# The gate products of a recurrent mixer as pairs of 64-row products in the two halves of the TensorE array

## The chip, the cores and the metric

The kernel runs on one core of a Trainium2 chip. The metric is the time of one launch on the device in microseconds (us), smaller is better. The median of the runs is what counts.

## The reference, cut to what matters

The reference is a decoder trunk of two layers on 512 positions of 1024 channels: FFN, token mixer and FFN in each layer, and a norm at the end. The change lies in the token mixer of layer 0, a gated linear recurrence:

```
def block_diag_linear(x, w, b):          # 16 heads of 64 channels
    xh = x.reshape(bsz, s, h, dh)
    return (jnp.einsum('bshi,hij->bshj', xh, w) + b).reshape(bsz, s, h * dh)
...
gate_a = sigmoid(block_diag_linear(x, w_a, b_a))
gate_x = sigmoid(block_diag_linear(x, w_x, b_x))
log_a = -8 * gate_a * softplus(-lam);  a = exp(log_a)
bx = x * gate_x * sqrt(-expm1(2 * log_a))
h[t] = a[t] * h[t-1] + bx[t]
```

Here x is the right half of `hn @ w_in` after a causal convolution of width 4. The left half goes through a GELU, is multiplied by h, and the product goes through `w_out`. Each head of 64 channels has a 64x64 matrix for gate a and one for gate x.

## The kernel before, in words

All matrices lie in single precision. To multiply them with TensorE's faster type, each operand is split into a high and a low part: ScalarE copies it to `hi` with rounding, VectorE subtracts to get `lo`, and three matmuls (hi·hi, lo·hi, hi·lo) sum into one PSUM bank (`mm3`, L242 to L245). Weights come by DMA into `raw` tiles and are split into `whi` and `wlo`; activations are split into tiles named `hi` and `lo` (`split`, L116).

The program is a list of steps (`subs`), each one block of weights. The loop at the end runs them in order. A step issues, on each engine in program order: the hooks of phase "pre", the split of the weights of the step three ahead, the hooks "mid" and "rest", the step's own matmuls, and then the hooks "end" and "late". Every engine works through its own queue in that order, so the place of a hook decides what stands behind what. A weight block must be split before its step's matmuls, and a bank must have been read before the next product is written to it. Six PSUM banks (`bank`) are given out in turn to the products and the gates.

The recurrent mixer (`recurrent`, L1198) is tiled by channel blocks c = 0..7 of 128 channels, two heads each, channels on the partitions and the 512 positions along the free dimension. Its first twelve steps make the right half of `hn @ w_in`. Blocks 0 to 3 come in two halves of 256 positions, blocks 4 to 7 in one step of 24 matmuls each (tile `r`). When block c is done, `r_post` (L1220) starts a chain over the following steps:

- ScalarE writes `rc` (the last tap of the convolution with its bias), and VectorE adds the other three taps (`taps`, "late").
- One step later ("mid") `rc` is split into `hi` and `lo`.
- At the end of that step or of the next one, `gate` puts two gate products on TensorE, one for a and one for x. Each uses a 128x128 weight tile with two heads' 64x64 matrices on its diagonal and zeros beside them, and each is three matmuls of 128 rows, 128 columns and 512 positions: 6 for a block, 48 in all. The weight tiles are made by `load_gate`: zeros from GpSimd, then DMAs into the diagonal blocks, four tiles of 128x512 in all, each split once (`split_gate`).
- One step after that ("mid") ScalarE takes the two `sigmoids` (tile `g`) with the gate's bias from the table of vectors `vec`, and a tanh of gate a (tile `tl`).
- Another step later VectorE multiplies `rc` by gate x (`product`, tile `pr`).

Within "mid" of one step, the sigmoids of an earlier block stand ahead of the split of a later block's `rc`. On TensorE gates 0, 1 and 2 each stand after the product of a later block, gates 3 and 4 back to back after block 5's, gate 5 after block 6's, and gates 6 and 7 back to back after the first product of the left half: six groups.

The recurrence itself is a list by hand (`plan`, L1301): `exp_` on ScalarE, `oma2` on VectorE (squares and products, tiles `a` and `tl`), square roots on ScalarE, `scan` on VectorE, GELUs on ScalarE, products `yh` on VectorE, and splits of them. They feed the product with `w_out`, seven products of a Strassen scheme with banks named A, B and C, that comes after the eight steps of the left half.

Of the kernel before, what the change touches and what calls it, by code (L numbers as in the profile page):

```python
# [11 lines left out]
AF = mybir.ActivationFunctionType  # L12
ALU = mybir.AluOpType

P = 128
# [10 lines left out]
V_F1, V_MIX, V_F2, V_CW, V_CB, V_GA, V_GX, V_LAM, V_SB = 0, 16, 32, 48, 80, 88, 96, 104, 112  # L26
# [44 lines left out]
def trunk(ctx: ExitStack, tc: tile.TileContext, a: dict, out: bass.AP):  # L71
    nc = tc.nc
# [28 lines left out]
    def f32(t):  # L101
        return t.bitcast(F32)

    def tt(o, x, y, op):
        nc.vector.tensor_tensor(out=o, in0=x, in1=y, op=op)  # L105
# [4 lines left out]
    def stt(o, x, s, y, op0, op1):  # L110
        nc.vector.scalar_tensor_tensor(out=o, in0=x, scalar=s, in1=y, op0=op0, op1=op1)  # L111

    def act(o, x, f, **k):
        nc.scalar.activation(out=o, in_=x, func=f, **k)  # L114

    def split(src):  # L116

        w = src.shape[-1]
        hi, lo = slot(F32R, "hi")[:, :w], slot(F32R, "lo")[:, :w]
        act(hi, src, AF.Copy)  # L120
        tt(lo, src, f32(hi), ALU.subtract)
        return hi, lo
# [110 lines left out]
    def hook(n, phase, fn):  # L233


        hooks.setdefault((n, phase), []).append(fn)
# [5 lines left out]
    def mm3(ps, wh, wl, xh, xl, start, stop):  # L242
        nc.tensor.matmul(ps, wh, xh, start=start, stop=False)  # L243
        nc.tensor.matmul(ps, wh, xl, start=False, stop=False)  # L244
        nc.tensor.matmul(ps, wl, xh, start=False, stop=stop)  # L245
# [17 lines left out]
    def vcol(row):  # L263
        return vec[:, row : row + 1]
# [933 lines left out]
    def recurrent(w_in, w_out, norm):  # L1198
        gates = {}

        def load_gate(name, q):
            g = gates[name, q] = slot(name="gw")
            nc.gpsimd.memset(g, 0.0)
            gv = g.rearrange("p (c j) -> p c j", c=4)
            wv = a[f"rec_gate_{name}_w"][0, q * 8 : (q + 1) * 8].rearrange("(c two) i j -> two i c j", two=2)
            for two in range(2):
                nc.sync.dma_start(out=gv[two * 64 : (two + 1) * 64, :, two * 64 : (two + 1) * 64], in_=wv[two])

        def split_gate(name, q):
            gates[name, q] = split(gates[name, q])  # L1210

        at0 = len(subs)
        y0 = at0 + 12
        for n, (name, q) in enumerate((name, q) for q in range(2) for name in ("a", "x")):
            hook(at0 + (-9,-8,-2,-1)[n], "late", lambda name=name, q=q: load_gate(name, q))
            hook(at0 + (-3,-2,3,4)[n], "mid", lambda name=name, q=q: split_gate(name, q))

        rc, ga, gx, tl, pr, ym = {}, {}, {}, {}, {}, {}

        def r_post(c, ps):  # L1220
            n = now[0]
            g = n + (2 if c < 4 or c == 6 else 1)
            v = rc[c] = slot(name="rc")
            hl, pss = [], []
            act(v, ps, AF.Identity, scale=vcol(V_CW + 24 + c), bias=vcol(V_CB + c))

            def taps():
                for k in (0, 1, 2):
                    stt(v[:, 3 - k :], ps[:, : T - 3 + k], vcol(V_CW + 8 * k + c), v[:, 3 - k :], ALU.mult, ALU.add)

            def gate():
                for name in "ax":
                    pg = bank("gate")
                    wh, wl = gates[name, c // 4]
                    cs = slice((c % 4) * P, (c % 4 + 1) * P)
                    mm3(pg, wh[:, cs], wl[:, cs], hl[0], hl[1], True, True)
                    pss.append(pg)
                hl.clear()

            def sigmoids():  # L1240
                for dst, brow in ((ga, V_GA), (gx, V_GX)):
                    dst[c] = slot(name="g")
                    act(dst[c], pss.pop(0), AF.Sigmoid, bias=vcol(brow + c))
                tl[c] = slot(name="tl")
                act(tl[c], ga[c], AF.Tanh, scale=lru_c[:, c : c + 1])

            def product():
                pr[c] = slot(name="pr")
                tt(pr[c], rc.pop(c), gx.pop(c), ALU.mult)

            hook(n, "late", taps)
            hook(n + 1, "mid", lambda: hl.extend(split(v)))
            hook(g, "end", gate)
            hook(g + 1, "mid", sigmoids)
            hook(g + 2, "mid", product)

# [272 lines left out]
    def lru_consts():  # L1529
# [44 lines left out]
        for i in range(13, 0, -2):  # L1574
# [73 lines left out]
    def vec_rest():  # L1648

        nc.vector.memset(stage[:V_ROWS, :P], 0.0)  # L1650
        for src, r0, n in rows:
            flat = src.rearrange("h d -> (h d)") if len(src.shape) == 2 else src.rearrange("o h d -> (o h d)")
            nc.gpsimd.dma_start(out=stage[r0 : r0 + n, :P], in_=flat.rearrange("(n p) -> n p", p=P))

    def vec_rest_t():
        ps = aux("vec")
# [146 lines left out]
```

## Time and profile before

| what | value |
|---|---|
| time, median of 3 runs | 1561.8 us (1561.55 to 1561.82) |
| the profiled execution, first to last instruction | 1559.5 us |
| instructions | 21004 |
| TensorE matmuls busy | 1551.9 us, 7293 matmuls |
| VectorE busy | 1309.5 us |
| ScalarE busy | 1188.7 us |
| GpSimd busy | 245.3 us |
| granted TensorE clock, mean | 0.999 |
| the recurrent mixer's gates on TensorE | from 350.9 to 392.0 us |

The profile holds one execution; of it the span is recorded and no other time, and the runs' median lies 2.3 us above that span. In the views PE is TensorE's matmuls, PEld its weight loads, DVE VectorE, ACT ScalarE, POOL GpSimd and SP the engine that issues most DMAs. A row of a timeline gives start, duration, engine, line, operation, output and inputs, shape and count, and in brackets the idle time of the engine before it with what ended it. Durations overlap: the next instruction of an engine starts before the one before has ended, so the cost of one among many is the distance between starts. Helpers hide lines (every ScalarE activation is L114), so tiles are the better guide.

### The profile page before, as it was taken

How to read it: one execution, taken by the hardware profiler on the slowest of the kernel's cores; microseconds unless marked ns; L12 is line 12 of the kernel's file. 1: busy time of each engine (PE TensorE's matmuls, PEld its weight loads, DVE VectorE, ACT ScalarE, POOL GpSimd, SP SyncE). 2: the span in 40 equal slices, each digit the busy share in tenths (PEclk: the TensorE clock that was granted, in tenths of full speed). 3: DMA queues.
4: the chain of work that ended last, by engine and by line, in shares of the span. 5: the costliest groups of instructions: out<-in, count | busy, mean ns of one | idle time of the engine just before them, and what ended most of it. 6: DMA issues, size and time to landing. Idle time of an engine off the chain costs nothing.

```text
span 1559.5 us, 21004 instructions
## 1 busy us (share of the span) xinstructions
PE 1551.9 (100%) x7293; PEld 1318.4 (85%) x7293; DVE 1309.5 (84%) x1776; ACT 1188.7 (76%) x1777; POOL 245.3 (16%) x220
## 2 busy tenths in 40 slices
PE   9999999999999999999999999999999999999998
PEld 7888888898888998888889988888888889888886
DVE  6977789888999777789897877798879997777998
ACT  7877787668778868796877787867787877778856
POOL 2111112300020111112211111122211111111220
PEclk9999999999999999999999999999999999999999
DMA  9888899953395988899977888989878859898994
GB/s 315 189 189 196 186 217 229 228 137 109 103 230 137 191 199 198 189 232 224 244 179 183 188 203 185 227 227 238 224 191 219 203 138 216 197 212 177 241 235 138
DMA packets 268763, 310.53 MB, mean 199 GB/s; under 512 B 111232, under 2 KB 149232, under 8 KB 268656
## 3 DMA queue, kind: packets, MB, share of 16 engines
q1 hardware_dynamic: 214368, 210.02, 46.4%
q0 software_dynamic: 52496, 97.33, 37.0%
q10 hardware_dynamic: 1792, 1.84, 0.4%
q8 instruction: 57, 0.93, 0.2%
q14 instruction: 50, 0.41, 0.1%
HBM read 282.39 MB, written 2.10 MB: 182 GB/s over the span
## 4 chain that ended last, share of the span: by engine, by line
PE 98%; DVE 1%; DMA 0%; ACT 0%; issue 0%; SPq 0%; DVEq 0%
PE A L479 15%; PE A L478 15%; PE A L480 15%; PE C L480 8%; PE C L479 8%; PE C L478 8%; PE B L479 4%; PE B L480 4%; PE B L478 4%; PE r L243 2%; PE r L244 2%; PE r L245 2%; PE Q L480 2%; PE Q L479 2%; PE Q L478 2%; PE p L958 1%
## 5 line engine op out<-in xcount | busy, mean ns | idle before, releaser
L105 DVE TENSOR_TENSOR wlo<-raw,whi 128x1024 fp32r<-128x1024 f32 (+2 forms) x567 | 651.9, 1153 | 208.3 <-ACT whi L114 206.7
L114 ACT ACTIVATE whi<-raw 128x1024 fp32r<-128x1024 f32 (+2 forms) x567 | 564.4, 1001 | 239.0 <-DVE raw L105 93.1
L478 PE MATMUL A<-whi,hi 128*128 128x512 f32 (+1 forms) x1104 | 421.0, 381 | 0.0
L479 PE MATMUL A<-whi,lo 128*128 128x512 f32 (+1 forms) x1104 | 419.3, 380 | 0.1
L480 PE MATMUL A<-wlo,hi 128*128 128x512 f32 (+1 forms) x1104 | 419.3, 380 | 0.0
L478 PEld LDWEIGHTS A<-whi,hi 128*128 128x128 f32 x1104 | 207.3, 188 | 35.9 <-ACT c L114 1.0
L480 PEld LDWEIGHTS A<-wlo,hi 128*128 128x128 f32 x1104 | 207.2, 188 | 35.6
L479 PEld LDWEIGHTS A<-whi,lo 128*128 128x128 f32 x1104 | 207.3, 188 | 35.4 <-DVE lo L105 0.5
L156 POOL DMA_DIRECT2D raw<-in_ffn_w_in_dram x100 | 120.7, 1207 | 710.1 <-DVE raw L105 322.8
L478 PE MATMUL C<-whi,hi 128*128 128x512 f32 (+1 forms) x608 | 231.4, 381 | 0.0
L479 PE MATMUL C<-whi,lo 128*128 128x512 f32 (+1 forms) x608 | 231.3, 380 | 0.0
L480 PE MATMUL C<-wlo,hi 128*128 128x512 f32 (+1 forms) x608 | 231.3, 380 | 0.0
L156 POOL DMA_DIRECT2D raw<-in_ffn_w_out_dram x73 | 83.8, 1194 | 319.1 <-DVE wlo L105 199.2
L105 DVE TENSOR_TENSOR raw<-raw,raw 128x1024 f32<-128x1024 f32 (+1 forms) x113 | 131.0, 1159 | 1.1
L479 PEld LDWEIGHTS C<-whi,lo 128*128 128x128 f32 x608 | 114.1, 188 | 20.1 <-DVE lo L105 0.2
L478 PEld LDWEIGHTS C<-whi,hi 128*128 128x128 f32 x608 | 114.2, 188 | 19.9
L480 PEld LDWEIGHTS C<-wlo,hi 128*128 128x128 f32 x608 | 114.1, 188 | 19.9
L105 DVE TENSOR_TENSOR lo<-a,hi 128x512 fp32r<-128x512 f32 (+1 forms) x184 | 119.7, 658 | 1.4 <-ACT hi L114 1.3
L114 ACT ACTIVATE hi<-a 128x512 fp32r<-128x512 f32 (+1 forms) x184 | 107.8, 596 | 14.5 <-DVE a L105 12.8
L114 ACT ACTIVATE c<-A 128x512 f32<-128x512 f32 (+1 forms) x150 | 81.9, 567 | 46.5 <-PE A L480 46.1
L479 PE MATMUL B<-whi,lo 128*128 128x512 f32 (+1 forms) x304 | 115.7, 381 | 0.2 <-DVE lo L111 0.2
L478 PE MATMUL B<-whi,hi 128*128 128x512 f32 (+1 forms) x304 | 115.7, 381 | 0.0
(189 smaller groups left out, 1964.5 us busy)
## 6 DMA issues: line engine op xcount, KB each, us to landing
raw<-in_ffn_w_in_dram SPq DMA_DIRECT2D x143, 512.0 KB, 5.6
raw<-in_ffn_w_out_dram SPq DMA_DIRECT2D x98, 512.0 KB, 5.7
raw<-in_ffn_w_in_dram POOLq DMA_DIRECT2D x76, 512.0 KB, 7.7
raw<-in_ffn_w_out_dram POOLq DMA_DIRECT2D x58, 512.0 KB, 7.6
raw<-in_ffn_w_in_dram SPq DMA_DIRECT2D x48, 384.0 KB, 4.2
raw<-in_sg_w_in_dram SPq DMA_DIRECT2D x20, 512.0 KB, 7.0
raw<-in_ffn_w_in_dram POOLq DMA_DIRECT2D x24, 384.0 KB, 6.3
raw<-in_rec_w_in_dram SPq DMA_DIRECT2D x16, 512.0 KB, 5.4
```

Source lines behind the costliest of these rows:

```text
L105: nc.vector.tensor_tensor(out=o, in0=x, in1=y, op=op)
L114: nc.scalar.activation(out=o, in_=x, func=f, **k)
L156: nc.gpsimd.dma_start(out=self.v, in_=src, accum_op=ALU.add)
L243: nc.tensor.matmul(ps, wh, xh, start=start, stop=False)
L244: nc.tensor.matmul(ps, wh, xl, start=False, stop=False)
L245: nc.tensor.matmul(ps, wl, xh, start=False, stop=stop)
L478: nc.tensor.matmul(ps, zh, wh, start=fresh and i == 0, stop=False, **k)
L479: nc.tensor.matmul(ps, zl, wh, start=False, stop=False, **k)
L480: nc.tensor.matmul(ps, zh, wl, start=False, stop=end, **k)
L958: nc.tensor.matmul(bank_of(half, s), z, (sub.lo if m == 2 else sub.hi)[:, q, :], start=left[2] == "2" and (h, q, m) == (0, 0, 0), stop=lef ...
```

## The change

The a and x matrices of one head are put side by side: a weight tile now has, in its rows 0 to 63, the even head's a in columns 0 to 63 and its x in columns 64 to 127, and in its rows 64 to 127 the odd head's x in columns 0 to 63 and its a in columns 64 to 127. There are no zeros left, so GpSimd's memsets go, and two weight tiles take the place of four, with two splits instead of four. A block's six gate matmuls become three pairs: the even head with rows 0 to 63 of the array into one bank, the odd head with rows 64 to 127 into another. Each has 64 rows, 128 columns and 512 positions. A bank now holds a and x of one head, so each gate is gathered by two activations of 64 partitions each: for a from the same partitions, for x from the other half. So there are four sigmoids for a block instead of two. The bias of gate x lies in `vec` with its halves exchanged, by two small DMAs at the start. The four gate DMAs of one half of the heads are issued at one place.

```
-                for name in "ax":
-                    pg = bank("gate")
-                    wh, wl = gates[name, c // 4]
-                    cs = slice((c % 4) * P, (c % 4 + 1) * P)
-                    mm3(pg, wh[:, cs], wl[:, cs], hl[0], hl[1], True, True)
-                    pss.append(pg)
+                pss.extend(bank("gate") for _ in range(2))
+                cs = slice((c % 4) * P, (c % 4 + 1) * P)
+                for m in range(3):
+                    for two in range(2):
+                        rows = slice(two * 64, (two + 1) * 64)
+                        nc.tensor.matmul(pss[two], gates[c // 4][m == 2][rows, cs], hl[0][m == 1][rows, :],
+                                         start=m == 0, stop=m == 2)
                 hl.clear()
 
             def sigmoids():
-                for dst, brow in ((ga, V_GA), (gx, V_GX)):
-                    dst[c] = slot(name="g")
-                    act(dst[c], pss.pop(0), AF.Sigmoid, bias=vcol(brow + c))
+                for dst, brow, n in ((ga, V_GA, 0), (gx, V_GX, 1)):
+                    g = dst[c] = slot(name="g")
+                    for two in range(2):
+                        o = (two ^ n) * 64
+                        act(g[two * 64 : (two + 1) * 64], pss[two][o : o + 64], AF.Sigmoid, bias=vcol(brow + c)[o : o + 64])
+                pss.clear()
...
-            g = gates[name, q] = slot(name="gw")
-            nc.gpsimd.memset(g, 0.0)
+            g = gates[q] = slot(name="gw")
...
-            for two in range(2):
-                nc.sync.dma_start(out=gv[two * 64 : (two + 1) * 64, :, two * 64 : (two + 1) * 64], in_=wv[two])
+            for n, name in enumerate("ax"):
+                wv = a[f"rec_gate_{name}_w"][0, q * 8 : (q + 1) * 8].rearrange("(c two) i j -> two i c j", two=2)
+                for two in range(2):
+                    o = (two ^ n) * 64
+                    nc.sync.dma_start(out=gv[two * 64 : (two + 1) * 64, :, o : o + 64], in_=wv[two])
...
-        for n, (name, q) in enumerate((name, q) for q in range(2) for name in ("a", "x")):
-            hook(at0 + (-9,-8,-2,-1)[n], "late", lambda name=name, q=q: load_gate(name, q))
-            hook(at0 + (-3,-2,3,4)[n], "mid", lambda name=name, q=q: split_gate(name, q))
+        for q in range(2):
+            hook(at0 + (-9, -2)[q], "late", lambda q=q: load_gate(q))
+            hook(at0 + (-3, 3)[q], "mid", lambda q=q: split_gate(q))
```

On TensorE, gate 0 (tiles `gate`, inputs `hi` and `lo` of `rc` and the split gate weights) stands before as two products of three matmuls, one bank after the other:

```order
L243 MATMUL gate_3463<-hi_3394,hi_3112 128x512
L244 MATMUL gate_3463<-lo_3395,hi_3112 128x512
L245 MATMUL gate_3463<-hi_3394,lo_3113 128x512
L243 MATMUL gate_3467<-hi_3394,hi_3134 128x512
L244 MATMUL gate_3467<-lo_3395,hi_3134 128x512
L245 MATMUL gate_3467<-hi_3394,lo_3135 128x512
```

Now it stands as three pairs, the two banks in turn, and both products read the same weight tile (`hi_3110`, `lo_3111`), one in its upper and one in its lower rows:

```order
L1239 MATMUL gate_3450<-hi_3381,hi_3110 128x512
L1239 MATMUL gate_3451<-hi_3381,hi_3110 128x512
L1239 MATMUL gate_3450<-lo_3382,hi_3110 128x512
L1239 MATMUL gate_3451<-lo_3382,hi_3110 128x512
L1239 MATMUL gate_3450<-hi_3381,lo_3111 128x512
L1239 MATMUL gate_3451<-hi_3381,lo_3111 128x512
```

The number of matmuls and their columns are as before; `lo` is first read by the third matmul of a block instead of the second.

On ScalarE, the stretch from block 5's `rc` (`rc_3644`) over the sigmoids of blocks 3 and 4 to the split of that `rc` reads before:

```order
L114 ACTIVATE rc_3644<-r_3603,vec 128x512
L114 ACTIVATE whi_3650<-raw_3094 128x1024
L114 ACTIVATE g_3656<-gate_3628,vec 128x512
L114 ACTIVATE g_3658<-gate_3632,vec 128x512
L114 ACTIVATE tl_3660<-g_3656,lru_c 128x512
L114 ACTIVATE g_3662<-gate_3636,vec 128x512
L114 ACTIVATE g_3664<-gate_3640,vec 128x512
L114 ACTIVATE tl_3666<-g_3662,lru_c 128x512
L114 ACTIVATE hi_3668<-rc_3644 128x512
```

And now, from the sigmoids on (the `rc` is `rc_3637`):

```order
L114 ACTIVATE g_3649<-gate_3621,vec 64x512
L114 ACTIVATE g_3649<-gate_3622,vec 64x512
L114 ACTIVATE g_3652<-gate_3621,vec 64x512
L114 ACTIVATE g_3652<-gate_3622,vec 64x512
L114 ACTIVATE tl_3655<-g_3649,lru_c 128x512
L114 ACTIVATE g_3657<-gate_3629,vec 64x512
L114 ACTIVATE g_3657<-gate_3630,vec 64x512
L114 ACTIVATE g_3660<-gate_3629,vec 64x512
L114 ACTIVATE g_3660<-gate_3630,vec 64x512
L114 ACTIVATE tl_3663<-g_3657,lru_c 128x512
L114 ACTIVATE hi_3665<-rc_3637 128x512
```

Four activations more stand ahead of the split of block 5 (`hi_3665`); all else keeps its order.

More of the change, by code (lines that the diff above doesn't have):

```diff
@@ L1199, in recurrent, with load_gate, split_gate @@
         gates = {}
-        def load_gate(name, q):
-            g = gates[name, q] = slot(name="gw")
-            nc.gpsimd.memset(g, 0.0)
+        def load_gate(q):
+            g = gates[q] = slot(name="gw")
             gv = g.rearrange("p (c j) -> p c j", c=4)
-            wv = a[f"rec_gate_{name}_w"][0, q * 8 : (q + 1) * 8].rearrange("(c two) i j -> two i c j", two=2)
-            for two in range(2):
-                nc.sync.dma_start(out=gv[two * 64 : (two + 1) * 64, :, two * 64 : (two + 1) * 64], in_=wv[two])
-        def split_gate(name, q):
-            gates[name, q] = split(gates[name, q])
+            for n, name in enumerate("ax"):
[3 more added lines that the diff above has]
+                    nc.sync.dma_start(out=gv[two * 64 : (two + 1) * 64, :, o : o + 64], in_=wv[two])
+        def split_gate(q):
+            gates[q] = split(gates[q])
         at0 = len(subs)
         y0 = at0 + 12
-        for n, (name, q) in enumerate((name, q) for q in range(2) for name in ("a", "x")):
-            hook(at0 + (-9,-8,-2,-1)[n], "late", lambda name=name, q=q: load_gate(name, q))
-            hook(at0 + (-3,-2,3,4)[n], "mid", lambda name=name, q=q: split_gate(name, q))
+        for q in range(2):
+            hook(at0 + (-9, -2)[q], "late", lambda q=q: load_gate(q))
+            hook(at0 + (-3, 3)[q], "mid", lambda q=q: split_gate(q))
         rc, ga, gx, tl, pr, ym = {}, {}, {}, {}, {}, {}
@@ L1251, in r_post @@
             hook(n, "late", taps)
-            hook(n + 1, "mid", lambda: hl.extend(split(v)))
+            hook(n + 1, "mid", lambda: hl.append(split(v)))
             hook(g, "end", gate)
@@ L1652, in vec_rest @@
             flat = src.rearrange("h d -> (h d)") if len(src.shape) == 2 else src.rearrange("o h d -> (o h d)")
-            nc.gpsimd.dma_start(out=stage[r0 : r0 + n, :P], in_=flat.rearrange("(n p) -> n p", p=P))
+            v = flat.rearrange("(n p) -> n p", p=P)
+            if r0 == V_GX:
+                for o in (0, 64):
+                    nc.gpsimd.dma_start(out=stage[r0 : r0 + n, o : o + 64], in_=v[:, 64 - o : 128 - o])
+            else:
+                nc.gpsimd.dma_start(out=stage[r0 : r0 + n, :P], in_=v)
     def vec_rest_t():
```

## The prediction, made before the changed kernel was run

> **What bounds the kernel now.** I read the page first: the busy times and the chain that ended last.
>
> ```profile
> span 1559.5 us, 21004 instructions
> PE 1551.9 (100%) x7293; PEld 1318.4 (85%) x7293; DVE 1309.5 (84%) x1776; ACT 1188.7 (76%) x1777; POOL 245.3 (16%) x220
> PE 98%; DVE 1%; DMA 0%; ACT 0%; issue 0%; SPq 0%; DVEq 0%
> ```
>
> TensorE carries the end nearly everywhere, so a shorter gate product looks like time won, one for one. But shares of the whole say little of one stage, so next I read the windows of 10 us over the mixer (columns: window, length, then busy time and count of PE, PEld, DVE, ACT, POOL).
>
> ```profile
> 370.00:380.00 10.00, 10.00 (x46) 8.28 (x45) 7.24 (x10) 9.97 (x16) 0.00 (x0) 1.00 0.52 126
> 380.00:390.00 10.00, 10.00 (x46) 8.29 (x45) 9.80 (x14) 8.44 (x12) 1.20 (x1) 1.00 0.22 58
> 400.00:410.00 10.00, 10.00 (x46) 8.29 (x45) 9.83 (x13) 8.86 (x11) 0.00 (x0) 1.00 0.15 50
> 430.00:440.00 10.00, 10.00 (x46) 8.29 (x45) 10.00 (x16) 6.51 (x9) 1.73 (x2) 1.00 1.02 217
> ```
>
> Here three engines are close to full: ScalarE for 9.97 of 10 us while gates 3 to 5 run, and then VectorE, up to 10.00 of 10. Before the change TensorE never waits, but those two have almost no room. The change takes work from TensorE and gives work to ScalarE, so the question is how much delay ScalarE can take.
>
> **TensorE's part.** The tile view of the gates and the timeline of PE:
>
> ```profile
> L243 PE MATMUL gate<-hi,hi x16: 389/389/396, 350.9 to 391.3; 128*128 128x512 f32 x16
> 368.88 0.39 PE L243 MATMUL gate<-hi,hi 128*128 128x512 f32 x1
> 371.60 0.39 PE L243 MATMUL r<-zh,whi 128*128 128x512 f32 x1
> ```
>
> Gates 3 and 4, twelve matmuls, take 371.60 − 368.88 = 2.72 us, 0.227 each by the distance of starts; a block's six take 1.36, all 48 take 10.9. If the two halves run side by side, a pair costs 0.227 and 24 × 0.227 = 5.4 us are saved. If they don't, 48 × 0.227 stays as it is. No row shows the array in halves, so both are ends. Going into and out of halves, a matmul may have to finish first: 0.389 − 0.227 = 0.16 us, and twelve times that (six groups) is 1.9 us more. So PE's term lies between −5.4 and +1.9. The Trainium skill, TensorEngine Tiling (Array Packing), section Theoretical Speedup, promises up to twofold for a contraction of 64 rows or less; by it alone the sum would be 1561.8 − 5.4 = 1556.4. The same page, Key Properties, says that changing the tiling mode drains TensorE; it gives no price. Which end is right matters little, as the next part shows.
>
> **ScalarE's part.** Each block gets two activations more, 16 in all, on 64 partitions by 512 columns:
>
> ```profile
> L114 ACT ACTIVATE g<-gate,vec x16: 672/688/704, 356.1 to 399.3; 128x512 f32<-128x512 f32 x16
> 356.08 1.27 ACT L114 ACTIVATE g<-gate,vec 128x512 f32<-128x512 f32 x2
> 357.24 0.72 ACT L114 ACTIVATE tl<-g,lru_c 128x512 f32<-128x512 f32 x1
> 361.73 0.65 ACT L114 ACTIVATE hi<-rc 128x512 fp32r<-128x512 f32 x1
> 362.96 1.05 ACT L114 ACTIVATE whi<-raw 128x1024 fp32r<-128x1024 f32 x1
> ```
>
> Two sigmoids hold the engine for 357.24 − 356.08 = 1.16, 0.58 each. No activation of 64 partitions is in the trace. The rows of 512 and 1024 columns (0.65 and 1.05) show that time goes with columns, and the columns stay 512; so I take the same price, 1.15 us more a block. The bounds: half of it (0.29 each, nothing added), and the whole duration without overlap (0.69 each, 1.6 us more a block).
>
> Now place by place, with what ScalarE waits for in between:
>
> ```profile
> 356.54 0.47 PE L243 MATMUL r<-zh,whi 128*128 128x512 f32 x1
> 354.07 2.31 DVE L111 SCALAR_TENSOR_TENSOR rc<-r,vec,rc 128x509 f32<-128x509 f32 x3
> 366.10 0.64 ACT L114 ACTIVATE hi<-rc 128x512 fp32r<-128x512 f32 x1 [0.32 <-DVE rc L111]
> 369.08 0.78 ACT L114 ACTIVATE rc<-r,vec 128x512 f32<-128x512 f32 x1 [2.35 <-PE r L245]
> 370.71 1.25 ACT L114 ACTIVATE g<-gate,vec 128x512 f32<-128x512 f32 x2
> 372.46 1.27 ACT L114 ACTIVATE g<-gate,vec 128x512 f32<-128x512 f32 x2
> 374.21 0.65 ACT L114 ACTIVATE hi<-rc 128x512 fp32r<-128x512 f32 x1
> 374.89 0.69 DVE L105 TENSOR_TENSOR lo<-rc,hi 128x512 fp32r<-128x512 f32 x1 [0.95 <-ACT hi L114]
> ```
>
> *Gates 0 to 3.* What PE wins at gates 0 and 1 is lost again at once: block 4's product (356.54) takes the bank whose taps end at 354.07 + 2.31 = 356.38, and these hang on VectorE, not on PE. Only 0.16 of room is there.
>
> *Gate 4.* Its `hi` (366.10) stands behind the sigmoids of blocks 0 to 2: 3 × 1.15 − 0.32 = 3.13 later, so from 369.23 to 369.87, and `lo` follows for 0.69, to 370.6. PE, with gates 2 and 3 shorter, could be there at 370.24 − 1.36 − 0.16 = 368.7 and now waits. Its second and third pair (0.45 together side by side, 0.9 otherwise) start at 370.6 and end at 371.05 to 371.5. Before it was 371.60: almost all won by then is gone.
>
> *Gate 5.* The 2.35 us that ScalarE idled before 369.08 swallow most of the 3.13 (back to back, `rc` starts 0.54 after `hi`, at 369.77, which is 0.69 late). Then come two blocks of sigmoids, 2.30: `hi` starts at 374.21 + 2.99 = 377.20, ends at 377.85, `lo` ends at 378.57.
>
> ```profile
> 377.04 0.39 PE L243 MATMUL gate<-hi,hi 128*128 128x512 f32 x1
> 378.40 0.39 PE L243 MATMUL r<-zh,whi 128*128 128x512 f32 x1
> 382.28 1.27 ACT L114 ACTIVATE g<-gate,vec 128x512 f32<-128x512 f32 x2
> 384.57 0.78 ACT L114 ACTIVATE rc<-r,vec 128x512 f32<-128x512 f32 x1
> 385.38 2.32 DVE L111 SCALAR_TENSOR_TENSOR rc<-r,vec,rc 128x509 f32<-128x509 f32 x3
> 389.35 0.68 DVE L105 TENSOR_TENSOR lo<-rc,hi 128x512 fp32r<-128x512 f32 x1
> 392.00 0.39 PE L243 MATMUL r<-zh,whi 128*128 128x512 f32 x1
> ```
>
> PE's last two pairs start at 378.6 and end at 379.05 to 379.5, against 378.40: now 0.65 to 1.1 late.
>
> *Gates 6 and 7.* From 374.21 to 384.57 no ScalarE row has idle time ahead of it, and block 5's sigmoids (382.28) add 1.15: `rc` of block 7 is 4.14 late, and with it VectorE's taps (385.38) and the `lo` of block 7 (389.35), which ends at 389.35 + 0.68 + 4.14 = 394.17. Gate 7's last two pairs end at 394.65 to 395.1 instead of 392.00: PE 2.65 to 3.1 late.
>
> *VectorE after that.* It has no idle time in the recurrence to give the delay back, and one wait is added:
>
> ```profile
> 396.96 1.27 ACT L114 ACTIVATE g<-gate,vec 128x512 f32<-128x512 f32 x2
> 398.73 1.26 ACT L114 ACTIVATE g<-gate,vec 128x512 f32<-128x512 f32 x2
> 401.91 0.72 ACT L114 ACTIVATE g<-g,lru_nc 128x512 f32<-128x512 f32 x1
> 404.38 0.67 DVE L105 TENSOR_TENSOR a<-g 128x512 f32<-128x512 f32 x1
> 418.47 0.63 ACT L114 ACTIVATE hi<-a 128x512 fp32r<-128x512 f32 x1 [5.54 <-DVE a L105]
> 439.75 0.68 DVE L105 TENSOR_TENSOR lo<-a,hi 128x512 fp32r<-128x512 f32 x1
> 441.18 0.39 PE L479 MATMUL C<-whi,lo 128*128 128x512 f32 x1
> ```
>
> The sigmoids of blocks 6 and 7 add 2.30 on ScalarE, so the exponential (401.91) is 6.44 late and ends at 409.07; VectorE's square of it (404.38), otherwise 4.14 late at 408.52, starts at 409.1: VectorE is 4.72 late. ScalarE recovers in its idle 5.54 us (418.47), VectorE doesn't. The `lo` at 439.75 ends at 440.43; the matmul that reads it started at 441.18. With 4.72 it ends at 445.15, so that matmul starts at 445.18, 4.0 late, and TensorE, 2.65 to 3.1 late by itself, waits there once more. Behind that the steps go as before, 4.0 later.
>
> **What goes at nothing.** Two splits of gate weights, four memsets and the earlier order of four small DMAs lie before 343 us, off the path: TensorE has its blocks split three steps ahead there. Their price if that cover were gone, and their gain, is at most what two splits hold, under 1.4 us.
>
> ```profile
> L114 ACT ACTIVATE hi<-gw x4: 614/637/656, 323.6 to 341.9; 128x512 fp32r<-128x512 f32 x4
> ```
>
> One more DMA into the table of vectors at the start adds nothing, since the first gate runs at 350.9.
>
> **The sum.** 1559.5 + 4.0 = 1563.5 for the execution; the runs' median lies 2.3 above that span, so 1561.8 + 4.0 = 1565.8 us. Overlap of the array's halves and its switches move TensorE's own part, not this: VectorE's `lo` sets it in both cases. Were the exponential not late, 4.14 − 0.75 = 3.4 would be left of the 4.0; with none of the room at the C matmul, 4.7.
>
> **The rivals.**
>
> *Half-price sigmoids* (other side: not slower). If 64 partitions cost half, ScalarE is as it was. TensorE then gains at gates 2 to 7, but not freely: ScalarE's `rc` at 369.08 hangs on PE and moves by 0.16 + 0.68 = 0.84 with it, VectorE behind it as well, and the `lo` before 441.18 has 0.75 of room. So the most is 0.84 + 0.75 = 1.6 us: 1560.2. For it speaks nothing in the trace, against it that time goes with columns. It decides from about 0.4 us an activation downward, where blocks add under 0.5 us and the idle 2.35 and 0.32 take it.
>
> *A price between*, about 0.5 us: each block adds 0.84 instead of 1.15, six blocks 1.9 less on VectorE, so 4.0 − 1.9 = 2.1: 1563.9. The 0.58 already contains the overlap of neighbours, so I give it little.
>
> *TensorE's gain is kept.* If the halves overlap and neither ScalarE nor VectorE sets the pace, 5.4 us go: 1556.4. The chain's 98% on PE speaks for it; 9.97 and 10.00 in the windows and the 0.16 us of room at block 4 against it. The Trainium skill's page TensorEngine Tiling (Array Packing), section PSUM Bottleneck, warns that faster products leave the reading of PSUM as it is; here the change even doubles that reading's instructions, and by that rule the gain would not be kept.
>
> *Dear halves.* At 0.69 each, six blocks delay VectorE by 6 × 0.46 = 2.8 more and the exponential, with 8 × 0.46 = 3.7 on ScalarE by then, VectorE by 0.9 beyond that: 1565.8 + 3.7 = 1569.5.
>
> **How the numbers follow.** Forecast 0.62, half price 0.12, a price between 0.15, gain kept 0.05, dear halves 0.06. A measurement of this kernel tells 0.2%, 3.1 us, from no change: slower means above 1564.9, faster below 1558.7. The forecast and the dear halves are slower: 0.68. Half price and the price between are within: 0.27. Faster: 0.05. The range of 1562.0 to 1568.5 leaves out half price, the kept gain and the end of the dear halves, 0.2 in all.
>
> **What the profile afterwards would show.** Right: 32 rows of `g` from `gate` on 64x512 at about 0.69; TensorE with waits, which it lacks now, at gates 4, 5 and 7 on `hi` and `lo` and at the C matmul on `lo`; windows of 360 to 380 us with ScalarE near full; the first C matmul some 4 us later than before, counted from gate 0. Pairs of gate matmuls starting closer than 0.2 us would show the overlap. Wrong: `g` rows near 0.4 us, no waits of TensorE on `hi` or `lo`, or a first C matmul that is not later.

## The result, and the profile after

The changed kernel takes 1569.6 us (median of 4 runs, 1569.44 to 1570.46), the kernel before 1561.8 us in the same set of runs (4 runs, 1561.55 to 1563.87). The ratio is 1.0050, with a 95% interval of 1.0037 to 1.0062: slower by 7.8 us. The forecast was 1565.8 us, slower by 4.0.

The page of the changed kernel, its span, busy times and chain that ended last:

```profile
span 1568.0 us, 21014 instructions
PE 1553.3 (99%) x7293; PEld 1314.4 (84%) x7293; DVE 1308.5 (83%) x1774; ACT 1199.2 (76%) x1791; POOL 243.2 (16%) x217
PE 91%; DVE 4%; ACT 3%; issue 1%; DMA 1%; SPq 0%; DVEq 0%; ACTq 0%
```

The chain, 98% on TensorE before, now has 7% on VectorE and ScalarE. ScalarE's busy time grew by 10.5 us. Among TensorE's waits on these two engines (tile and line that waited, who released it: us in total, times, longest), those at the gates and at the C product are new; `lo` is the remainder that VectorE takes of ScalarE's rounded copy `hi`:

```profile
PE gate L1239 <- ACT hi L114: 3.3, 2, 1.8
PE gate L1239 <- DVE lo L105: 1.6, 3, 1.1
PE C L479 <- DVE lo L105: 0.6, 1, 0.6
```

The window in which gates 4 and 5 wait shows who is full there (columns as in the prediction: PE, PEld, DVE, ACT, POOL):

```profile
370.00:380.00 10.00, 7.19 (x34) 4.91 (x30) 5.46 (x8) 9.80 (x15) 0.09 (x1) 1.00 0.65 160
```

From 370 to 380 us TensorE is busy for 7.19 of 10 us, where it was for 10.00, while ScalarE stays near full with 9.80.

**TensorE's pairs.** The timeline of PE around gate 0:

```profile
351.11 0.28 PE L245 MATMUL r<-zh,wlo 128*128 128x256 f32 x1
351.32 0.51 PE L1239 MATMUL gate<-hi,hi 64*128 64x512 f32 x2
351.66 0.40 PE L1239 MATMUL gate<-lo,hi 64*128 64x512 f32 x2
351.89 0.40 PE L1239 MATMUL gate<-hi,lo 64*128 64x512 f32 x2
352.23 0.39 PE L243 MATMUL r<-zh,whi 128*128 128x256 f32 x1
352.45 0.28 PE L244 MATMUL r<-zl,whi 128*128 128x256 f32 x1
```

The two halves of the array do work side by side: the two matmuls of a pair together last 0.51 us, where one lasts 0.50, and pairs start 0.34 and 0.23 apart. The group of gate 0 takes 352.23 − 351.32 = 0.91 us instead of the prediction's 1.36. Going in costs 351.32 − 351.11 = 0.21 where 256 columns otherwise take 0.12 (so 0.09), and the next matmul after the halves holds the array for 0.22 instead of 0.12 (0.10). Within the group the first and the last pair hold it for 0.34 instead of 0.23, 0.11 more each. So a group pays some 0.4 us for going in and out, and a block by itself gains no more than 0.3 us all told. The Trainium skill, TensorEngine Tiling (Array Packing), section Theoretical Speedup, has up to twofold for this; the trace agrees for the pairs, and the group as a whole gets 1.5.

**ScalarE's sigmoids.** The tile view of the gates (duration in ns: least, median, most):

```profile
L114 ACT ACTIVATE g<-gate,vec x32: 666/683/687, 356.4 to 410.0; 64x512 f32<-64x512 f32 x32
```

The first block on the timeline of ACT:

```profile
356.42 2.80 ACT L114 ACTIVATE g<-gate,vec 64x512 f32<-64x512 f32 x4
359.24 0.72 ACT L114 ACTIVATE tl<-g,lru_c 128x512 f32<-128x512 f32 x1
360.39 0.76 ACT L114 ACTIVATE rc<-r,vec 128x512 f32<-128x512 f32 x1
```

A half sigmoid lasts 0.683 us, a whole one 0.688 before: half the partitions save nothing. But where two whole ones held the engine for 1.16 us, four half ones hold it for 359.24 − 356.42 = 2.82, or 0.705 each. They do not overlap at all. A block adds 1.66 us, where the prediction had 1.15.

**Where TensorE falls behind.** Gates 4 and 5, and what follows gate 5, on the timeline of PE (idle time before an instruction and its releaser in brackets):

```profile
371.68 0.51 PE L1239 MATMUL gate<-hi,hi 64*128 64x512 f32 x2 [1.43 <-ACT hi L114]
372.40 0.50 PE L1239 MATMUL gate<-lo,hi 64*128 64x512 f32 x2 [0.22 <-DVE lo L105]
373.07 0.50 PE L243 MATMUL r<-zh,whi 128*128 128x512 f32 x1
380.68 0.51 PE L1239 MATMUL gate<-hi,hi 64*128 64x512 f32 x2 [1.84 <-ACT hi L114]
381.41 0.50 PE L1239 MATMUL gate<-lo,hi 64*128 64x512 f32 x2 [0.22 <-DVE lo L105]
382.07 0.53 PE L243 MATMUL r<-zh,whi 128*128 128x512 f32 x1
382.41 0.61 PE L244 MATMUL r<-zl,whi 128*128 128x512 f32 x1
385.81 0.41 PE L243 MATMUL r<-zh,whi 128*128 128x512 f32 x1
```

The first product after gate 4 comes at 373.07 (371.60 before), the one after gate 5 at 382.07 (378.40 before). Eight matmuls then fill 385.81 − 382.41 = 3.40 us, 0.425 each instead of 0.227: TensorE's clock fell. The window of that stretch (PEclk is the last but two):

```profile
382.40:386.00 3.60, 3.60 (x10) 2.80 (x9) 2.86 (x5) 3.60 (x7) 0.00 (x0) 0.53 0.00 0
```

The granted clock was 0.53 there. The last places are gate 7 and the C product of the output matrix, with the exponential that makes VectorE late in between:

```profile
397.53 0.50 PE L1239 MATMUL gate<-lo,hi 64*128 64x512 f32 x2 [1.12 <-DVE lo L105]
398.19 0.50 PE L243 MATMUL r<-zh,whi 128*128 128x512 f32 x1
412.70 1.95 ACT L114 ACTIVATE g<-g,lru_nc 128x512 f32<-128x512 f32 x3
413.46 0.69 DVE L105 TENSOR_TENSOR a<-g 128x512 f32<-128x512 f32 x1 [1.50 <-ACT g L114]
448.85 0.69 DVE L105 TENSOR_TENSOR lo<-a,hi 128x512 fp32r<-128x512 f32 x1
449.60 0.50 PE L479 MATMUL C<-whi,lo 128*128 128x512 f32 x1 [0.57 <-DVE lo L105]
```

Gate 7 is left at 398.19 (392.00 before). The square behind the exponential starts at 413.46 (404.38 before), and the C matmul at 449.60 (441.18 before), 8.4 later; from there to the end nothing is added. In this execution 0.4 us of that were there at 7 us already (the warm-up matmul at 6.98, before at 6.58), long ahead of the change, so 8.0 belong to it, against 7.8 by the runs.

```profile
6.98 0.38 PE L1646 MATMUL warm<-warm 128*128 128x512 bf16 x1
```

### The profile page after: what moved, and what is told of

The parts are those of the page before. It is cut to its first block, busy times and chain, and to the rows that moved or that the text cites. A ratio compares the mean times of both kernels' runs of the same rounds, so it can differ in the third digit from the quotient of the medians.

```text
span 1568.0 us, 21014 instructions
## 1 busy us (share of the span) xinstructions
PE 1553.3 (99%) x7293; PEld 1314.4 (84%) x7293; DVE 1308.5 (83%) x1774; ACT 1199.2 (76%) x1791; POOL 243.2 (16%) x217
## 3 DMA queue, kind: packets, MB, share of 16 engines
q10 hardware_dynamic: 1792, 1.84, 0.4%
## 4 chain that ended last, share of the span: by engine, by line
PE 91%; DVE 4%; ACT 3%; issue 1%; DMA 1%; SPq 0%; DVEq 0%; ACTq 0%
PE A L480 15%; PE A L479 15%; PE A L478 15%; PE C L479 8%; PE C L480 8%; PE C L478 8%; PE B L479 4%; PE B L480 4%; PE B L478 4%; ACT g L114 2%; PE Q L480 2%; PE Q L478 2%; PE Q L479 2%; PE p L958 1%; DVE wlo L105 1%; PE e L289 1%
```

## The experiments

The leading theory, S: the time goes on ScalarE, because the half sigmoids are dearer than whole ones, and everything behind is the predicted chain of waits. The rival, A: the products in the array's halves cost it. Each experiment starts from the kernel before or from the changed one, as its expectation says. The first four shared their runs of the kernel before (1561.86 us, 21 runs), so did the next three (1561.34, 15 runs); the last had its own (1561.90, 8 runs).

**The pairs alone.** The changed kernel's products, with whole sigmoids over each bank:

```
-                for dst, brow, n in ((ga, V_GA, 0), (gx, V_GX, 1)):
-                    g = dst[c] = slot(name="g")
-                    for two in range(2):
-                        o = (two ^ n) * 64
-                        act(g[two * 64 : (two + 1) * 64], pss[two][o : o + 64], AF.Sigmoid, bias=vcol(brow + c)[o : o + 64])
-                pss.clear()
+                for dst, brow in ((ga, V_GA), (gx, V_GX)):
+                    dst[c] = slot(name="g")
+                    act(dst[c], pss.pop(0), AF.Sigmoid, bias=vcol(brow + c))
```

> The changed kernel's 64-row products, but each of a block's two banks is read by one sigmoid of all 128 partitions, as before the change; a and x of the two heads are then mixed up, so the output is not the reference's. Theory S (the loss is ScalarE's price for sigmoids of half the partitions): ScalarE's queue is the old one, TensorE no longer waits on hi or lo at the gates, and the time is a little under that of before, by 0.5 to 1.6 us (1560.2 to 1561.3); the shorter products can't give more since VectorE sets the pace at the C matmul. Theory A (the loss comes from the 64-row products: entering and leaving the halves, the fallen clock behind them): still slower than before, by 3 us or more.

Measured: 1560.82 us (11 runs), ratio 0.9991 (0.9982 to 1.0000). The pairs cost nothing, and they also bring next to nothing, though TensorE's work shrinks by some 2.9 us: four groups of one block by 0.25 to 0.3 us each, switches included, and the two of two blocks by 0.93 each (from the last matmul ahead of gate 3 to the second one behind gate 4 it takes 371.05 − 368.81 = 2.24 instead of 371.82 − 368.65 = 3.17; gates 1, 6 and 7, where TensorE waits, are taken as the same). TensorE's waits tell where that went:

```profile
PE gate L1239 <- DVE lo L105: 0.7, 1, 0.7
PE r L243 <- DVE rc L111: 0.6, 1, 0.6
PE C L479 <- DVE lo L105: 0.3, 1, 0.3
```

The bank of block 4's product, the remainder of gate 7 and the remainder at the C product each take a piece back, as the prediction said of TensorE's gain. A is out.

**Half sigmoids alone, by turns.** The kernel before, its products whole, each sigmoid cut in two:

```
-                    dst[c] = slot(name="g")
-                    act(dst[c], pss.pop(0), AF.Sigmoid, bias=vcol(brow + c))
+                    g, ps = slot(name="g"), pss.pop(0)
+                    dst[c] = g
+                    for two in range(2):
+                        r = slice(two * 64, (two + 1) * 64)
+                        act(g[r], ps[r], AF.Sigmoid, bias=vcol(brow + c)[r])
```

> The kernel before with its own 128-row products; only each sigmoid is cut into two of 64 partitions (lower, then upper half, in and out at the same partitions). The output is the reference's. Theory S: the four sigmoids take 2.80 us a block as in the changed kernel, and the time is that of the changed kernel, 1569.5, give or take 0.7. Theory A: within 1.5 us of before, 1560.3 to 1563.3.

Measured: 1570.45 us (5 runs), ratio 1.0051 (1.0038 to 1.0064), 0.25 above what S gave. The half sigmoids alone make the whole loss, and TensorE waits for the copy `hi` at the gates for 3.8 us in all. The first block on the timeline of ACT, its sigmoids as in the changed kernel, and the `rc` behind it:

```profile
356.33 2.79 ACT L114 ACTIVATE g<-gate,vec 64x512 f32<-64x512 f32 x4
360.42 0.78 ACT L114 ACTIVATE rc<-r,vec 128x512 f32<-128x512 f32 x1
```

**Half sigmoids in runs.** The same four, but both lower halves first, then both upper halves, so that two neighbours stay on the same partitions:

```
+                ga[c], gx[c] = slot(name="g"), slot(name="g")
+                for two in range(2):
+                    r = slice(two * 64, (two + 1) * 64)
+                    for g, ps, brow in ((ga[c], pss[0], V_GA), (gx[c], pss[1], V_GX)):
+                        act(g[r], ps[r], AF.Sigmoid, bias=vcol(brow + c)[r])
```

> As the run before it, but a block's four half sigmoids stand as lower of a, lower of x, upper of a, upper of x, so that two of the neighbouring pairs have the same partitions. Theory S1 (an activation of 64 partitions never overlaps the next): 0.70 each as with turns, 2.80 us a block, 1569.5. Theory S2 (only a change of the partitions between neighbours costs the overlap): starts 0.58 and 0.70 apart in turn, about 2.55 us a block, and some 2 us less in time: 1567.5.

Measured: 1568.76 us (5 runs, 1568.05 to 1571.61), ratio 1.0042 (1.0029 to 1.0056). The first block on the timeline of ACT:

```profile
358.39 0.68 ACT L114 ACTIVATE g<-gate,vec 64x512 f32<-64x512 f32 x1
358.98 0.68 ACT L114 ACTIVATE g<-gate,vec 64x512 f32<-64x512 f32 x1
359.67 0.68 ACT L114 ACTIVATE g<-gate,vec 64x512 f32<-64x512 f32 x1
360.25 0.67 ACT L114 ACTIVATE g<-gate,vec 64x512 f32<-64x512 f32 x1
```

The starts lie 0.59, 0.69 and 0.58 apart. On the same partitions two neighbours overlap as whole ones do; where the partitions change, the overlap of 0.1 us is gone. That is why the half sigmoids were dearer. The time is 1.3 us above S2's 1567.5, and the step down from the run before, 1.7 us, is within what the two intervals leave open; the distances of the starts are what shows it.

**Four whole sigmoids.** The kernel before, each whole sigmoid done twice, by turns of a and x. This is as many activations as the change has, at the prediction's price:

```
+                ga[c], gx[c] = slot(name="g"), slot(name="g")
+                for _ in range(2):
+                    for g, ps, brow in ((ga[c], pss[0], V_GA), (gx[c], pss[1], V_GX)):
+                        act(g, ps, AF.Sigmoid, bias=vcol(brow + c))
```

> The kernel before with its own products; each block's two sigmoids of 128 partitions are done twice (a, x, a, x), so 16 activations are added at the price that the prediction took. The output is the reference's. If the prediction's chain of waits is right and only the price of a half sigmoid was wrong: starts 0.58 apart and the prediction's own sum, 1565.8, within 3.4 to 4.7 us over before (1565.2 to 1566.5). If the chain itself is wrong (the delay has other ways through): outside of that, and near 1569 if the number of activations alone makes the loss.

Measured: 1565.67 us (11 runs), ratio 1.0023 (1.0014 to 1.0031). The first block's four last 2.42 us together, 0.57 to 0.58 from start to start, and the C matmul waits for the same remainder of VectorE, on the timelines of ACT and PE:

```profile
356.41 2.42 ACT L114 ACTIVATE g<-gate,vec 128x512 f32<-128x512 f32 x4
445.47 0.50 PE L479 MATMUL C<-whi,lo 128*128 128x512 f32 x1 [0.40 <-DVE lo L105]
```

It starts 4.3 us later than before; 0.33 of these were there at gate 0 already (351.22, before 350.89), so 4.0 belong to the sigmoids, as in the prediction (445.18). The time stands at the forecast's 1565.8. At the price that the prediction took, its chain of waits on ScalarE and VectorE comes out as written; gate 4, which the prediction had waiting, does not wait with TensorE's products whole. Only the price was wrong.

**What has to agree: the rows written.** The changed kernel, its half sigmoids in the order a lower, x lower, x upper, a upper. The two of a pair then write the same partitions and read different ones. The expectation names the last two the other way round; as the lines stand, the second and the third share neither the rows they read nor those they write:

```
+                ga[c], gx[c] = slot(name="g"), slot(name="g")
+                for h, n in ((0, 0), (0, 1), (1, 1), (1, 0)):
+                    g, brow, o = (ga[c], V_GA, h * 64) if n == 0 else (gx[c], V_GX, (1 - h) * 64)
+                    act(g[h * 64 : (h + 1) * 64], pss[h][o : o + 64], AF.Sigmoid, bias=vcol(brow + c)[o : o + 64])
```

> The changed kernel with the four half sigmoids of a block in another order: a's lower half and x's lower half (both written to partitions 0 to 63, read from the lower and the upper rows of the first bank), then a's upper half and x's upper half (both written to partitions 64 to 127, read from the upper and the lower rows of the second bank). So the first and the second, and the third and the fourth, share only the partitions that they write; the second and the third share only those that they read. In the changed kernel as it is, one pair of neighbours of each block already shares the rows that it reads and not those that it writes, and starts 0.70 us apart like the others. Theory O (what decides the overlap is the partitions that are written): starts about 0.58, 0.70, 0.58 apart, a block's four sigmoids take about 2.55 us in place of 2.80, and the time comes down as from the half sigmoids by turns to those in runs, by 1 to 2 us, to 1567.5 to 1568.8. Theory B (both read and written partitions have to agree): all starts 0.70 apart, 2.80 us a block, 1569.2 to 1570.0, the time of the changed kernel.

Measured: 1570.40 us (5 runs), ratio 1.0058 (1.0045 to 1.0070), 0.4 above B's range.

```profile
356.06 2.78 ACT L114 ACTIVATE g<-gate,vec 64x512 f32<-64x512 f32 x4
358.87 0.72 ACT L114 ACTIVATE tl<-g,lru_c 128x512 f32<-128x512 f32 x1
```

The four take 358.87 − 356.06 = 2.81 us, and every start is 0.69 to 0.70 after the one before: to write the same partitions is not enough (theory O falls). These pairs also read one bank, which left a doubt that the last experiment removes.

**The waits at the gates, without ScalarE's load.** The changed kernel with the rounding copy of the next block moved between a's and x's half sigmoids (`sigmoids` is cut into `first` and `second`):

```
-            hook(n + 1, "mid", lambda: hl.append(split(v)))
+            L = hooks.setdefault((n + 1, "mid"), [])
+            at = [i for i, f in enumerate(L) if f.__name__ == "first"][:1]
+            L.insert(at[0] + 1 if at else len(L), lambda: hl.append(split(v)))
...
-            hook(g + 1, "mid", sigmoids)
+            hook(g + 1, "mid", first)
+            hook(g + 1, "mid", second)
```

> The changed kernel with one thing moved on ScalarE: the copy that rounds the recurrence's next block (hi from rc) and on which the gate products wait now stands between a's two half sigmoids and x's two of an earlier block, where it stood behind all four and the hyperbolic tangent. No work is added or taken away. Theory W (the time is lost where TensorE stands waiting: 3.3 us at the gates for ScalarE's copy, about 0.5 for VectorE's remainder of it, and 1.7 in the low clock that follows the longest of these waits): those waits and the low clock go, and the time falls by 3 to 5 us, to 1564.5 to 1566.5. Theory L (what counts is ScalarE's load: its exponentials for blocks 0 to 4 come no earlier, so VectorE's work behind them and the C product that waits for its remainder at about 449 us come no earlier either): the gates' waits get shorter, the low clock may go, but the wait at the C product, 0.6 us in the changed kernel, grows by as much, to 3 to 5 us, and the time stays at 1569 to 1570.3.

Measured: 1571.75 us (5 runs), ratio 1.0063 (1.0051 to 1.0076). W falls: the long waits at gates 4 and 5 went and no time came back. L was right in that, but not on the place or the size. The waits came back at gates 6 and 7, not at the C product, and the time is above L's 1570.3. Gates 4, 5 and 7 on the timeline of PE:

```profile
371.76 0.50 PE L1239 MATMUL gate<-lo,hi 64*128 64x512 f32 x2 [0.41 <-DVE lo L105]
378.09 0.50 PE L1239 MATMUL gate<-hi,hi 64*128 64x512 f32 x2
397.03 0.80 PE L1239 MATMUL gate<-hi,hi 64*128 64x512 f32 x2 [4.18 <-ACT hi L114]
```

Gate 5 starts at 378.09 with no wait instead of 380.68, and gate 7 then waits 4.18 us. ScalarE is the reason, on its own timeline:

```profile
363.55 0.63 ACT L114 ACTIVATE hi<-rc 128x512 fp32r<-128x512 f32 x1 [0.21 <-DVE rc L111]
364.21 1.39 ACT L114 ACTIVATE g<-gate,vec 64x512 f32<-64x512 f32 x2
382.93 3.18 ACT L114 ACTIVATE g<-g,lru_nc 128x512 f32<-128x512 f32 x5
396.34 0.63 ACT L114 ACTIVATE hi<-rc 128x512 fp32r<-128x512 f32 x1 [1.50 <-DVE rc L111]
```

Ahead of sigmoids, the copy waits 0.21 us for the taps and takes 364.21 − 363.55 = 0.66 instead of 0.52, as the half sigmoid behind it does not overlap with it. The exponentials of blocks 0 to 4, at 381.94 in the changed kernel, start at 382.93, and the last copy, at 395.23 there, at 396.34. What TensorE no longer waits for at gates 4 and 5 it waits for at gates 6 and 7. The clock fell again, now with the wait of 4.18 us, and it stays low until about 404 us:

```profile
396.00:402.00 6.00, 4.16 (x11) 2.61 (x12) 5.89 (x10) 4.32 (x6) 0.00 (x0) 0.50 0.79 175
```

**Is it a matter of PSUM?** The kernel before with each hyperbolic tangent, which reads SBUF, cut in two:

```
-                act(tl[c], ga[c], AF.Tanh, scale=lru_c[:, c : c + 1])
+                for r in (slice(0, 64), slice(64, P)):
+                    act(tl[c][r], ga[c][r], AF.Tanh, scale=lru_c[r, c : c + 1])
```

> The kernel before, its sigmoids whole, but each of the eight hyperbolic tangents behind them cut into partitions 0 to 63 and 64 to 127; they read and write the same partitions, both in SBUF, where the sigmoids read PSUM. Whole, a tangent starts 0.57 us after the sigmoid ahead of it and the next work starts 0.61 after it. Theory G (an activation that works on other partitions than the one ahead of it never overlaps with it, whatever it reads): the second half starts 0.68 to 0.73 us after the first, so ScalarE's part of a block grows by about 0.8 us (0.7 for the added instruction and 0.1 for the boundaries around it), some 6 us over the eight, and the time is 1563 to 1565, less than the 1565.7 of two added whole sigmoids. Theory M (the lost overlap belongs to reads of PSUM): the second half starts 0.57 to 0.61 us after the first, a block grows by 0.57 to 0.6, and the time is 1562.2 to 1563.5; the distance of the starts decides.

Measured: 1563.34 us (10 runs), ratio 1.0010 (1.0001 to 1.0020). The first block on the timeline of ACT:

```profile
356.15 1.27 ACT L114 ACTIVATE g<-gate,vec 128x512 f32<-128x512 f32 x2
357.31 0.71 ACT L114 ACTIVATE tl<-g,lru_c 64x512 f32<-64x512 f32 x1
358.03 0.72 ACT L114 ACTIVATE tl<-g,lru_c 64x512 f32<-64x512 f32 x1
358.78 0.63 ACT L114 ACTIVATE hi<-rc 128x512 fp32r<-128x512 f32 x1
```

The second half starts 0.72 after the first, and the next whole activation 0.75 after the second, where a whole tangent is followed after 0.61. G holds for the upper half and for the whole behind it: the overlap is lost in SBUF as well. It does not hold for the lower half behind a whole one: the two whole sigmoids hold the engine for 357.31 − 356.15 = 1.16 us, as they did ahead of a whole tangent. So it may be the first partition that has to agree and not the set of them; no run has a whole activation behind a lower half, which would tell. A block grows by 358.78 − 357.31 − 0.61 = 0.86 us.

**Different banks.** As the half sigmoids in runs, but x's halves are read crosswise:

```
+                lo, hi = slice(0, 64), slice(64, P)
+                for g, ps, brow, w, r in ((ga[c], pss[0], V_GA, lo, lo), (gx[c], pss[1], V_GX, lo, hi),
+                                          (ga[c], pss[0], V_GA, hi, hi), (gx[c], pss[1], V_GX, hi, lo)):
+                    act(g[w], ps[r], AF.Sigmoid, bias=vcol(brow + c)[r])
```

> The kernel before with each whole sigmoid cut in halves as in the half sigmoids in runs (a lower, x lower, a upper, x upper by what they write), but x's two halves are read from the other half of its bank, so that gate x's two heads are swapped in the output. Neighbours read different banks throughout; the first two and the last two write the same partitions and read different ones, and the second and the third read the same partitions and write different ones. In the run with shared written partitions, such neighbours read the same bank as well. Theory B (both the partitions read and those written have to agree): every start is 0.68 to 0.72 us after the one before, a block takes about 2.8 us, and the time is that of the half sigmoids by turns, 1569.5 to 1571. Theory K (in that run it was the same bank that kept the neighbours apart): starts 0.58, 0.70 and 0.58 apart, about 2.55 us a block, and 1568 to 1569.5.

Measured: 1569.80 us (8 runs), ratio 1.0045 (1.0034 to 1.0057).

```profile
356.36 2.79 ACT L114 ACTIVATE g<-gate,vec 64x512 f32<-64x512 f32 x4
359.17 0.73 ACT L114 ACTIVATE tl<-g,lru_c 128x512 f32<-128x512 f32 x1
```

Four take 359.17 − 356.36 = 2.81 us, 0.70 each, whether neighbours share only the rows they write (the first two, the last two) or only those they read (the second and the third). Both have to agree. K falls.

What ScalarE was given more of, and what it cost, in one table: the time from the first block's first sigmoid to the next `rc`, as growth over the 358.37 − 356.08 = 2.29 us of the kernel before, and the time as a difference of the medians of one set of runs. The run with the copy moved ahead has its `rc` at another place and is left out.

| run | ScalarE more per block, us | time more, us |
|---|---|---|
| halved tangents | 0.87 | 2.0 |
| four whole sigmoids | 1.14 | 3.8 |
| half sigmoids in runs | 1.54 | 6.9 |
| different banks | 1.66 | 7.9 |
| the changed kernel | 1.68 | 7.8 |
| the rows written | 1.79 | 9.1 |
| half sigmoids by turns | 1.80 | 8.6 |

The time goes with ScalarE's load, with the array in halves or without. Between 0.87 and 1.80 it grows by 7 to 8 us for each us a block, close to one for one over eight blocks; below that, ScalarE's and VectorE's idle times take part of it.

Three runs have a further 0.12 us a block that is not in the sigmoids. By turns, in runs and in the rows written, `rc` starts 0.64 to 0.65 us after the copy `hi` ahead of it once half sigmoids have run, in the other runs 0.51 to 0.55 (360.42 − 359.77 by turns, 360.39 − 359.87 in the changed kernel). In those three the last half sigmoid of a block reads the upper rows of its bank and of `vec`, in the changed kernel and with different banks the lower ones, and `rc` reads all rows of a bank, with a tangent and a copy from SBUF in between. So the overlap seems to hang on the last read of PSUM or of `vec` too; which of them, no run tells. Over six blocks it comes to 0.7 us, and by turns and the rows written lie 0.8 and 1.3 us above the changed kernel.

## Why the prediction was wrong in size

**TensorE's part: right.** The halves overlap, and going in and out costs some 0.4 us a group, rather more than the two times 0.16 of the sum. Of the two ends the sum could have taken the better one without any change to the result, as it said: with whole sigmoids the kernel comes out 1.0 us faster, not 2.9, and with half ones nothing of it is left.

**ScalarE's part: the step that failed.** "I take the same price, 1.15 us more a block." That columns count and partitions don't was right: 0.683 against 0.688 us. But the 0.58 contained an overlap with the neighbour, and the prediction carried that overlap over to neighbours on other partitions. They start 0.705 apart, a block adds 1.66, and the true value lay at the upper bound, "the whole duration without overlap". The Trainium skill, ScalarE: Activation LUTs, section What ACT_TABLE_LOAD costs, says that neighbouring activations overlap by about 93 ns; the whole sigmoids agree (0.688 − 0.58 = 0.11), the half ones on changing partitions do not.

**The places: right, with the other price.** The prediction's own steps, with 1.66 in place of 1.15, against the changed kernel less the 0.4 us that its execution had from the start:

- Gate 4: 3 × 1.66 − 0.32 = 4.66 instead of 3.13, so it ends 1.53 later than the forecast's 371.05 with pairs side by side, at 372.6. Measured 373.07 − 0.4 = 372.7.
- Gate 5: `rc` 0.69 + 1.53 = 2.22 late, two blocks of sigmoids 3.32, so 2.55 later than the forecast's 379.05: 381.6. Measured 382.07 − 0.4 = 381.7.
- Gate 7: the `rc` of block 7 is 2.22 + 3.32 + 1.66 = 7.20 late instead of 4.14, so 3.06 later than the forecast's 394.65: 397.7. Measured 398.19 − 0.4 = 397.8.
- The exponential: blocks 6 and 7 add 3.32 where the forecast had 2.30, so with the 3.06 it is 4.08 later than forecast. The square behind it, forecast at 409.1, comes at 413.2; measured 413.46 − 0.4 = 413.1.
- The C matmul: forecast at 445.18, with 4.08 more at 449.26. Measured 449.60 − 0.4 = 449.2.

So the sum would have been 4.0 + 4.08 = 8.1 and the time 1569.9; the runs gave 1569.6.

**What wasn't foreseen and cost nothing: the clock.** The eight slow matmuls hold TensorE 8 × (0.425 − 0.227) = 1.6 us longer. Yet the C matmul is where the sum without it puts it, since VectorE's remainder sets that matmul. This is argued from the sum, not tried by itself. The runs of the changed kernel fit it: one with a mean granted clock of 0.999 took 1569.73 us, two with 0.997 took 1569.44 and one with 0.996 took 1570.46, so down to 0.997 no price shows. In the run with the copy moved ahead it is otherwise: TensorE comes to that C matmul at 451.10 and waits for nothing there, as the remainder was ready at 449.94 + 0.68 = 450.62. So there TensorE's own delay, with the low clock from 394 to 404 us in it, sets the time. How much of the 10.4 us the clock makes stays open.

**The rivals.** Half price is out (0.683 us), and so is a price between. The kept gain is out: whole sigmoids with pairs gained 1.0 us (0 to 2.8 by the interval), not 5.4. The dear halves were the case, at 1569.5 by the prediction's own working, and were given 0.06. They should have had far more: the row that 0.58 came from was for neighbours on the same partitions, and none was for neighbours on different ones.

No run here beats the kernel before by more than its measurement can tell. The lowest, the pairs with whole sigmoids, is no version to use, as its expectation tells; it says that the products alone have about 0.1% to give, 0.2% at most.

## What to carry to other kernels

A duration between starts contains the overlap with the neighbour, and the overlap is known only for neighbours like those in the trace. When a change makes neighbours of another kind, such as halves of the partitions by turns, price them at the full duration, or keep that end at an equal chance. And when one engine is full, work that is taken from another buys nothing, and moving the full engine's instructions about only moves the waits.

## What the runs showed of the hardware

- An activation on 64 partitions lasts as long as one on 128 (0.683 and 0.688 us at 512 columns). Two neighbours start 0.57 to 0.59 us apart when both read and write the same partitions, and 0.69 to 0.75 when either differs, from PSUM or from SBUF, also from an upper half to a whole. A half that reads and writes the lower partitions keeps the overlap behind a whole one (0.58).
- Two matmuls of 64 rows in the array's two halves run side by side, at 0.23 us a pair in the middle of a group. Changing to halves and back costs about 0.2 us each way (0.09 and 0.11 going in, 0.11 and 0.10 coming out).
- In the changed kernel TensorE's clock fell to 0.53 for 3.4 us behind a wait of 1.84 and one of 0.22 us, but not behind one of 1.43 and one of 0.22. The length of the waits alone does not decide: in the run of the rows written it fell at gate 4 to 0.57 behind 1.53 and 0.23, and with half sigmoids by turns it stayed at 1.00 at gate 5 behind 1.59 and 0.22. The Trainium skill, TensorE: Matmul & The Clock Gate, section What's actually happening, tells of about 3.4 us without work before the clock is halved, and as much busy time before it is full again. The length of the changed kernel's slow stretch agrees; here waits of 1.8 us in sum were enough.
